# Rotary step of a decoder-trunk kernel: the partner rows added by accumulating transfers of the Pool queue

## Chip, cores and metric

The kernel runs on one core of a Trainium2 chip. The metric is the device time of one execution in microseconds (us). Each time below is that of the whole program: one layer of gated linear attention, one layer of dilated attention, two feed-forward blocks, for 1024 prompt tokens and 32 sample tokens.

## What is computed

The part that matters is the rotary step of keys and queries. Each head is a vector of 128 numbers per token. After its RMS norm, the first 32 of the 128 are rotated in pairs (number a with number a + 16) by an angle that depends on the token's position; the other 96 stay as they are.

```python
def rope_partial(x, pos):
    half = ROPE_DIM // 2                      # 16
    ...
    x1 = xf[..., :half]
    x2 = xf[..., half:ROPE_DIM]
    out = jnp.concatenate([x1 * cos - x2 * sin, x2 * cos + x1 * sin, xf[..., ROPE_DIM:]], axis=-1)

def dilated_mixer(h, w_q, q_norm, w_o, pos, attend):
    q = (h @ w_q).reshape(B, L, N_GROUPS, N_KV, Q_PER_KV, HEAD_DIM)
    q = rope_partial(rms_norm(q, q_norm), pos)
    for g, (win, dil) in enumerate(DIL_GROUPS):
        o, l = attend(q[:, :, g], win, dil)
```

Four key heads and 24 query heads (3 groups g of 8) are rotated this way, 28 heads in all. The rest of the trunk (projections, softmax, feed-forward) is not touched.

## The kernel before

Activations stand transposed: a tile has 128 partitions (features) and T = 1056 columns (1024 prompt tokens, 32 sample tokens), all float32. A projection of one head is 24 matmuls for each third of the columns (CW = 352): eight weight blocks, each as high and low part in three products (`proj`, L929 and L271).

`qk_head` (L793) finishes a head. For each third it scales the product (L829), squares it (L831), splits the square (L135), sums it over the partitions by two matmuls with ones (L800, L801), takes the reciprocal root by Ln and Exp on ScalarE (L802, L803), and writes the normed head on VectorE (L805). Heads of the groups g > 0 are written by L809 in class order: token 4u + r goes to column 256r + u, since the dilated attention works on the four classes r of the tokens; L813 writes the 32 sample columns. Then `rotate` (L815) turns the first 32 partitions, in four VectorE operations on 32 x 1056 elements: a shuffle that fetches the partner rows (L817), the product of the partner with the sine table (L818), the product of the head with the cosine table (L819), and the sum (L820). The tables are loaded by `rope_table` (L837): one in token order for keys and group 0, one in class order for groups 1 and 2, made on the host.

The steps of `qk_head` are put into a list `late` and run one third later, so a head's rotation is written while the next head is projected.

`mixer` (L1142 and on) runs eight slots s. In a slot, `attend(s)` (L957) takes the three queries q[0], q[1], q[2] of the slot:

- eight near-by scores of q[0] (L973) with their masked softmax parts on VectorE (L966) and exponentials on ScalarE,
- eight dilated scores (L984), each from q[1] and q[2], with the same softmax part (L966),
- weights that go through DRAM and back (L1005, L1007), transposes and products with the values (L1018 to L1056).

Score tiles come from a pool of two PSUM buffers (`sc`, L893): a score's matmul waits until the softmax part two scores before it has read its buffer. The queries of slot s + 1 are projected in between. After every second slot `sample` (L1069 and on) does the sample tokens' attention, from `Qs`, into which GpSimd copies the sample columns of each head (`sample_part`, L943).

Each engine does its instructions in a fixed order that a list scheduler of the framework sets when the program is built, from its own estimate of each operation's duration. A change of one operation thus also changes the place of others.

Names in the rows: `hs` is the temporary of `rotate`, `q` and `kh` are the heads, `tab` the tables, `p_s` the score tiles, `pA` and `pB` the near-by and dilated softmax tiles, `p_n` the sum of squares, `mm` a projection, `htl` and `hth` the low and high part of the square.

Of the kernel before, what the change touches and what calls it, by code (L numbers as in the profile page):

```python
# [8 lines left out]
F32 = mybir.dt.float32  # L9
# [4 lines left out]
ALU = mybir.AluOpType  # L14
# [4 lines left out]
NP, NS = 1024, 32  # L19
T = NP + NS  # L20
# [15 lines left out]
def yoco_step_kernel(  # L36
# [6 lines left out]
    nc = tc.nc  # L43
# [8 lines left out]
    class Turns:  # L52


        def __init__(self, *pools):
            self.pools, self.n = list(pools), 0
# [45 lines left out]
    def gcol(i):  # L102
        return gt[:, i:i + 1]

    G_A, G_F, G_E, G_KV, G_B, G_ON, G_K, G_Q, G_GK = 0, (8, 16), (24, 32), 40, 48, 56, 58, 59, 60

    XH, XL = [], []
# [24 lines left out]
    def split(hi, lo, x, g=None):  # L132
        if g is None:
            nc.scalar.copy(hi, x)  # L134
            nc.vector.tensor_tensor(lo, x, hi.bitcast(F32), op=ALU.subtract)  # L135
        else:
            nc.scalar.activation(hi, x, AF.Copy, scale=g)
            nc.vector.scalar_tensor_tensor(lo, x, g, hi.bitcast(F32), op0=ALU.mult, op1=ALU.subtract)  # L138
# [116 lines left out]
    def wtile(src, kt=8):  # L255
        raw = raws.tile([128, 1024], F32, tag="raw", name="raw")
        hi = wp.tile([128, 8, 128], F32R, tag="whi", name="whi")
        lo = wp.tile([128, 8, 128], F32R, tag="wlo", name="wlo")
        n = kt * 128
        nc.sync.dma_start(raw[:, :n], src)  # L260
        split(*(t[:].rearrange("p k m -> p (k m)")[:, :n] for t in (hi, lo)), raw[:, :n])
        return hi, lo
# [526 lines left out]
    def ln_exp_set():  # L789
        return tc.keep_in_program_order(nc.scalar.preload_act_table_set("natural_log_exp_and_others"))  # L790


    def qk_head(chunks, g, tab, tp, dst, pre, late, classes=False, early=False):  # L793
        def flush():
            while late:
                late.pop(0)()

        def finish(s, q, t, th, tl):
            p = sm.pools[0].tile([128, CW], F32, tag="sm", name="p_n")
            nc.tensor.matmul(p, ones_r, th, start=True, stop=False)  # L800
            nc.tensor.matmul(p, ones_r, tl, start=False, stop=True)  # L801
            nc.scalar.activation(t, p, AF.Ln, scale=1.0 / 128, bias=epsb)  # L802
            nc.scalar.activation(t, t, AF.Exp, scale=-0.5)  # L803
            if not classes:
                nc.vector.scalar_tensor_tensor(dst[:, s], q, g, t, op0=ALU.mult, op1=ALU.mult)  # L805
                return
            e = min(s.stop, NP) - s.start
            u = slice(s.start // 4, (s.start + e) // 4)
            nc.vector.scalar_tensor_tensor(  # L809
                dst[:, :NP].rearrange("p (r u) -> p u r", r=4)[:, u], q[:, :e].rearrange("p (u r) -> p u r", r=4), g,  # L810
                t[:, :e].rearrange("p (u r) -> p u r", r=4), op0=ALU.mult, op1=ALU.mult)
            if e < CW:
                nc.vector.scalar_tensor_tensor(dst[:, NP:], q[:, e:], g, t[:, e:], op0=ALU.mult, op1=ALU.mult)  # L813

        def rotate():  # L815
            t = tp.tile([64, T], F32, tag="hs", name="hs")
            nc.vector.stream_shuffle(t[32:64], dst[:32], [(a + 16) % 32 for a in range(32)])  # L817
            nc.vector.tensor_tensor(t[:32], t[32:64], tab[32:64], op=ALU.mult)  # L818
            nc.vector.tensor_tensor(dst[:32], dst[:32], tab[:32], op=ALU.mult)  # L819
            nc.vector.tensor_tensor(dst[:32], dst[:32], t[:32], op=ALU.add)  # L820

        for c, ps in chunks:
            flush()
            s = slice(c * CW, (c + 1) * CW)
            q, t, th, tl = (tp.tile([128, CW], F32R if n in ("hth", "htl") else F32, tag=n, name=n, bufs=3 if n == "hq" else 2)
                            for n in ("hq", "ht", "hth", "htl"))
            if early:
                nc.scalar.copy(q, ps)
            nc.vector.tensor_tensor(q, q if early else ps, rstd[:, s], op=ALU.mult)  # L829
            with tc.issue_after(pre.ins):  # L830
                nc.scalar.activation(t, q, AF.Square)  # L831
            split(th, tl, t)
            late.append(lambda a=(s, q, t, th, tl): finish(*a))
        late.append(rotate)
        return flush

    def rope_table(pool, i=0):  # L837
        tab = pool.tile([64, T], F32, name=f"tab{i}")
        nc.sync.dma_start(tab, c_rope[i])
        return tab  # L840


    def shared_kv(X, ssq, tp):
# [35 lines left out]
        return mq  # L879

    def to_class(ap):
        return ap.rearrange("p (u r) -> p r u", r=4)

    class Mixer:
        def __init__(self, st, mq):
            def pool(name, bufs, **k):
                return st.enter_context(tc.tile_pool(name=name, bufs=bufs, **k))

            self.mq = mq
            self.po = sm.pools[1]
            self.sc = pool("sc", 2, space=PSUM, side="right")  # L893
            self.tr = pool("tr", 1, space=PSUM, side="right")
            p = self.pool = pool("mx", 1)
            self.mask_a = p.tile([128, 256], F32, name="mask_a")
            self.mask_b = p.tile([128, 768], F32, name="mask_b")
            self.mask_s = p.tile([128, 656], F32, name="mask_s")
            self.Qs = [p.tile([128, 8, 32], F32, name=f"Qs{h}") for h in range(4)]
            self.kn = p.tile([128, 4, 32], F32, name="kn")  # L900
            self.os = p.tile([128, 8, 8, 4], F32, name="os")
            self.tab = [rope_table(p, i) for i in range(2)]
            self.head(0)
            self.pre = ln_exp_set()
            for h in range(4):
                nc.gpsimd.memset(self.Qs[h], 0.0)
# [33 lines left out]
        def queries(self, s):  # L940
            out, late = [], []

            def sample_part(g, q):  # L943
                nc.gpsimd.tensor_copy(
                    self.Qs[s // 2][:, :, g * 8 + s % 2 * 4:g * 8 + s % 2 * 4 + 4],
                    q[:, NP:].rearrange("p (b t) -> p b t", t=4))

            for g in range(3):
                q = self.pool.tile([128, T], F32, tag="q", name="q", bufs=QB)
                flush = qk_head(self.proj(wtile(w_q[3 * s + g]), XH, XL), gcol(G_Q), self.tab[g > 0], self.pool, q,  # L950
                                self.pre, late, classes=g > 0)
                late.append(lambda g=g, q=q: sample_part(g, q))
                out.append(q)
            flush()
            return out
# [234 lines left out]
    X, ssq, tp = block(0, xp, X, H_, L_, Od[7], w_oa, pick0)  # L1190
# [4 lines left out]
    xp, op, X = mixer(mq)  # L1195
# [141 lines left out]
```

## Time and profile before

| | us |
|---|---|
| median of 3 runs | 2961.36 (2958.55 to 2965.35) |
| profiled execution, device time | 2967.59 |
| its span, first to last instruction | 2965.8 |
| TensorE (PE) busy | 2909.5 |
| VectorE (DVE) busy | 1845.1 |
| ScalarE (ACT) busy | 1085.1 |
| GpSimd (POOL) busy | 19.9 |

The span is the time between the first and the last instruction; 1.8 us of the device time lie around it. Engines work side by side, so busy times do not add up to the span. The row of an engine tells how long it had something in work; a wait row tells how long it had nothing, and which other engine's result or which transfer ended that. PEld is TensorE's loading of weights, which runs beside the matmuls. A "wait of PE" is time without a running matmul, a "wait of PEld" time without a running weight load, during which an earlier matmul may still run.

### The profile page before, as it was taken

Reading aid. Unit: us, or ns where it says so; the run is one execution under the profiler, and the core shown is the slowest. Engines: PE = TensorE matmul, PEld = TensorE weight load, DVE = VectorE, ACT = ScalarE, POOL = GpSimd, SP = SyncE. Lnnn points to the kernel's source line nnn. Section 1 sums busy time; section 2 is a strip of 40 time slices with the busy share of each in tenths; the row PEclk is TensorE's granted clock in tenths of the full one; section 3 lists DMA queues with packets and bytes.
Section 4 is the critical chain, followed back from the end, with each engine's and each line's share of the span. In section 5 each row is a group of like instructions: output and inputs, shape, how many; then the busy total and the mean of one; then the engine's idle time right before and its main releaser. Section 6 shows DMA issues by size and latency. Waiting matters only on the chain.

```text
span 2965.8 us, 47230 instructions
## 1 busy us (share of the span) xinstructions
PE 2909.5 (98%) x19920; PEld 2762.0 (93%) x19920; DVE 1845.1 (62%) x2769; ACT 1085.1 (37%) x1761; POOL 19.9 (1%) x44
## 2 busy tenths in 40 slices
PE   8999999999999999999999999999999999999999
PEld 7889898899999999999988879788899999999999
DVE  6345455776766544467687778784676666654364
ACT  5233333522222221235455555552532222231141
POOL 0000000000000000000000000000000000000000
PEclk9999999999999999999999999999999999999999
DMA  3121234322222442132433141334422222262123
GB/s 129 59 74 51 74 140 142 119 80 80 81 72 87 171 129 74 41 127 102 132 91 107 59 122 44 115 107 134 167 79 73 87 72 80 76 237 75 50 77 110
DMA packets 133987, 291.06 MB, mean 98 GB/s; under 512 B 34160, under 2 KB 58736, under 8 KB 132752
## 3 DMA queue, kind: packets, MB, share of 16 engines
q1 hardware_dynamic: 133040, 287.72, 29.4%
q8 instruction: 157, 2.57, 0.4%
q14 instruction: 54, 0.44, 0.1%
q10 hardware_dynamic: 736, 0.33, 0.0%
HBM read 216.14 MB, written 71.86 MB: 97 GB/s over the span
## 4 chain that ended last, share of the span: by engine, by line
PE 88%; DVE 6%; DMA 3%; ACT 2%; issue 1%; SPq 0%; DVEq 0%; ACTq 0%
PE mm L271 38%; PE be L207 13%; PE ga L207 9%; PE al L207 8%; PE mm L937 6%; PE mm L671 2%; PE p_s L984 1%; PE p_o L1052 1%; PE mm L289 1%; DMA vv<-in_cv_dram 1%; DMA kk<-in_ck_dram 1%; DVE hs L817 1%; DVE q L809 1%; PE p_s L973 1%; DVE q L819 1%
## 5 line engine op out<-in xcount | busy, mean ns | idle before, releaser
L134 ACT CAST whi<-raw 128x1024 fp32r<-128x1024 f32 (+2 forms) x244 | 197.6, 810 | 789.3 <-PE mm L271 578.5
L135 DVE TENSOR_TENSOR wlo<-raw,whi 128x1024 fp32r<-128x1024 f32 (+2 forms) x244 | 224.6, 921 | 80.0 <-ACT whi L134 79.9
L764 DVE TENSOR_TENSOR X<-mm,X 128x1056 f32<-128x1056 f32 (+1 forms) x100 | 121.1, 1213 | 235.7 <-PE mm L271 235.5
L271 PE MATMUL mm<-XH,wlo 128*128 128x352 f32 x1104 | 245.3, 328 | 4.7 <-DVE wlo L135 4.7
L271 PE MATMUL mm<-XH,whi 128*128 128x352 f32 x1104 | 249.3, 331 | 0.2 <-ACT q_in L295 0.2
L271 PE MATMUL mm<-XL,whi 128*128 128x352 f32 x1104 | 247.3, 328 | 0.2 <-DVE XL L138 0.2
L134 ACT CAST hw<-S 128x512 fp32r<-128x512 f32 x176 | 108.8, 621 | 314.7 <-PE ga L207 181.8
L271 PE MATMUL mm<-GH,wlo 128*128 128x352 f32 x1038 | 223.6, 324 | 0.0
L271 PE MATMUL mm<-GL,whi 128*128 128x352 f32 x1038 | 223.6, 323 | 0.0
L271 PE MATMUL mm<-GH,whi 128*128 128x352 f32 x1038 | 223.3, 323 | 0.0
L207 PE MATMUL be<-Bh,hw 128*128 128x264 f32 x1056 | 216.6, 286 | 5.2 <-ACT hw L134 5.2
L207 PE MATMUL be<-Bl,hw 128*128 128x264 f32 x1056 | 215.8, 286 | 0.0
L207 PE MATMUL be<-Bh,lw 128*128 128x264 f32 x1056 | 214.9, 285 | 0.0
L271 PEld LDWEIGHTS mm<-XH,wlo 128*128 128x128 f32 x1104 | 189.0, 190 | 8.0 <-DVE wlo L135 5.3
L271 PEld LDWEIGHTS mm<-XH,whi 128*128 128x128 f32 x1104 | 188.6, 189 | 8.2 <-issue 3.1
L271 PEld LDWEIGHTS mm<-XL,whi 128*128 128x128 f32 x1104 | 190.2, 189 | 4.1 <-issue 1.3
L937 PE MATMUL mm<-XL,whi 128*128 128x352 f32 x576 | 193.7, 336 | 0.0
L937 PE MATMUL mm<-XH,whi 128*128 128x352 f32 x576 | 193.7, 336 | 0.0
L937 PE MATMUL mm<-XH,wlo 128*128 128x352 f32 x576 | 189.3, 329 | 0.0
L271 PEld LDWEIGHTS mm<-GL,whi 128*128 128x128 f32 x1038 | 177.0, 188 | 0.3 <-DVE GL L135 0.2
L271 PEld LDWEIGHTS mm<-GH,whi 128*128 128x128 f32 x1038 | 176.6, 188 | 0.0
L271 PEld LDWEIGHTS mm<-GH,wlo 128*128 128x128 f32 x1038 | 176.5, 189 | 0.0
(342 smaller groups left out, 6292.9 us busy)
## 6 DMA issues: line engine op xcount, KB each, us to landing
raw<-in_w_fi_dram SPq DMA_DIRECT2D x88, 512.0 KB, 3.5
Gd<-g SPq DMA_DIRECT2D x44, 528.0 KB, 2.7
gr<-Gd SPq DMA_DIRECT2D x44, 528.0 KB, 4.9
raw<-in_w_fo_dram SPq DMA_DIRECT2D x64, 256.0 KB, 2.7
raw<-in_w_a_dram SPq DMA_DIRECT2D x24, 512.0 KB, 3.5
raw<-in_w_q_dram SPq DMA_DIRECT2D x24, 512.0 KB, 3.7
kk<-in_ck_dram SPq DMA_DIRECT2D x40, 256.0 KB, 3.5
vv<-in_cv_dram SPq DMA_DIRECT2D x40, 256.0 KB, 2.9
```

Of the source, the lines that this page charges most:

```text
L134: nc.scalar.copy(hi, x)
L135: nc.vector.tensor_tensor(lo, x, hi.bitcast(F32), op=ALU.subtract)
L207: nc.tensor.matmul(ps[:, c, :HC], a[:, k, :], b[:, c * HC:(c + 1) * HC], start=(first and k == 0 and i == 0), stop=(k == len(xs) - 1 and i ...
L271: nc.tensor.matmul(ps[:, c, :CW], a[:, k, :], b[k][:, c * CW:(c + 1) * CW], start=(k == 0 and i == 0), stop=(k == n - 1 and i == 2),)
L289: nc.tensor.matmul(ps, a[:, k, :], b[k][:, s], start=(k == 0 and i == 0), stop=(k == n - 1 and i == 2))
L671: nc.tensor.matmul(ps[:, c, :CW], raw[:, 128 * k:128 * k + 128], ps_[k][:, c * CW:(c + 1) * CW], start=(k == 0), stop=(k == 1))
L764: nc.vector.tensor_tensor(like(X[m], s, p), p, like(X[m], s, p), op=ALU.add)
L809: nc.vector.scalar_tensor_tensor(dst[:, :NP].rearrange("p (r u) -> p u r", r=4)[:, u], q[:, :e].rearrange("p (u r) -> p u r", r=4), g, t[: ...
L817: nc.vector.stream_shuffle(t[32:64], dst[:32], [(a + 16) % 32 for a in range(32)])
L819: nc.vector.tensor_tensor(dst[:32], dst[:32], tab[:32], op=ALU.mult)
L937: nc.tensor.matmul(ps, a[:, k, :], b[k][:, s], start=(k == 0 and i == 0), stop=(k == n - 1 and i == 2))
L973: nc.tensor.matmul(ps[:, :n], q[0][:, j * 128:(j + 1) * 128], self.KA[:, k0:k0 + n], start=True, stop=True)
```

## The change

`rotate` keeps two VectorE products: partner table times head into `t`, and cosine table times head in place. The sum over the partner rows is made by two transfers of the Pool queue: rows 16 to 31 of `t` are added to rows 0 to 15 of the head, and rows 0 to 15 of `t` to rows 16 to 31. For that the sine table is loaded with its two halves swapped. The shuffle and the VectorE sum go. There is one table, in token order; heads in class order read it with a step of four columns, in one product of 1024 columns, and the 32 sample columns get a product of their own.

```diff
         def rotate():
-            t = tp.tile([64, T], F32, tag="hs", name="hs")
-            nc.vector.stream_shuffle(t[32:64], dst[:32], [(a + 16) % 32 for a in range(32)])
-            nc.vector.tensor_tensor(t[:32], t[32:64], tab[32:64], op=ALU.mult)
-            nc.vector.tensor_tensor(dst[:32], dst[:32], tab[:32], op=ALU.mult)
-            nc.vector.tensor_tensor(dst[:32], dst[:32], t[:32], op=ALU.add)
+            t = tp.tile([32, T], F32, tag="hs", name="hs")
+            for d, tb, own in ((t, tab[:, 1], False), (dst, tab[:, 0], True)):
+                if classes:
+                    nc.vector.tensor_tensor(*(x[:32, :NP].rearrange("p (r u) -> p r u", r=4) for x in (d, dst)),
+                                            to_class(tb[:, :NP]), op=ALU.mult)
+                    nc.vector.tensor_tensor(d[:32, NP:], dst[:32, NP:], tb[:, NP:], op=ALU.mult)
+                else:
+                    nc.vector.tensor_tensor(d[:32], dst[:32], tb, op=ALU.mult)
+            for i in range(2):
+                nc.gpsimd.dma_start(dst[16 * i:16 * i + 16], t[16 - 16 * i:32 - 16 * i], accum_op=ALU.add)
...
-    def rope_table(pool, i=0):
-        tab = pool.tile([64, T], F32, name=f"tab{i}")
-        nc.sync.dma_start(tab, c_rope[i])
+    def rope_table(pool):
+        tab = pool.tile([32, 2, T], F32, name="tab")
+        nc.sync.dma_start(tab[:, 0], c_rope[0, :32])
+        for i in range(2):
+            nc.sync.dma_start(tab[16 * i:16 * i + 16, 1], c_rope[0, 48 - 16 * i:64 - 16 * i])
         return tab
+
+    def to_class(ap):
+        return ap.rearrange("p (u r) -> p r u", r=4)
...
-            self.tab = [rope_table(p, i) for i in range(2)]
+            self.tab = rope_table(p)
...
-                flush = qk_head(self.proj(wtile(w_q[3 * s + g]), XH, XL), gcol(G_Q), self.tab[g > 0], self.pool, q,
+                flush = qk_head(self.proj(wtile(w_q[3 * s + g]), XH, XL), gcol(G_Q), self.tab, self.pool, q,
```

In the changed file the lines after `rotate` have other numbers: L966 becomes L975, L973 L982, L984 L993, L937 L946; the products are L820 (class order), L822 (sample columns) and L824, the transfers L826.

The scheduler also places other instructions differently. VectorE's order in slot s = 1, about the rotation of its last head q[2], before (`q_14134` is q[2]; the rows L966 with `pA` are the last near-by softmax parts):

```order
L966 ISA pA_14304,stA_14278<-p_s_14302,mask_a_13243 128x256
L966 ISA stA_14278 128x1
L809 SCALAR_TENSOR_TENSOR q_14134<-hq_14218,gt_72,ht_14219 128x88x4
L966 ISA pA_14309,stA_14278<-p_s_14307,mask_a_13243 128x256
L966 ISA stA_14278 128x1
L966 ISA pA_14314,stA_14278<-p_s_14312,mask_a_13243 128x256
L966 ISA stA_14278 128x1
L966 ISA pA_14319,stA_14278<-p_s_14317,mask_a_13243 128x256
L966 ISA stA_14278 128x1
L809 SCALAR_TENSOR_TENSOR q_14134<-hq_14257,gt_72,ht_14258 128x80x4
L813 SCALAR_TENSOR_TENSOR q_14134<-hq_14257,gt_72,ht_14258 128x32
L817 STREAM_SHUFFLE hs_14272<-q_14134 32x1056
```

The same place now (`q_14140` is q[2]):

```order
L975 ISA pA_14319,stA_14288<-p_s_14317,mask_a_13245 128x256
L975 ISA stA_14288 128x1
L809 SCALAR_TENSOR_TENSOR q_14140<-hq_14265,gt_72,ht_14266 128x80x4
L813 SCALAR_TENSOR_TENSOR q_14140<-hq_14265,gt_72,ht_14266 128x32
L820 TENSOR_TENSOR hs_14280<-q_14140,tab_13254 32x1024
L822 TENSOR_TENSOR hs_14280<-q_14140,tab_13254 32x32
L975 ISA pA_14324,stA_14288<-p_s_14322,mask_a_13245 128x256
L975 ISA stA_14288 128x1
L820 TENSOR_TENSOR q_14140<-q_14140,tab_13254 32x1024
L822 TENSOR_TENSOR q_14140<-q_14140,tab_13254 32x32
L975 ISA pA_14329,stA_14288<-p_s_14327,mask_a_13245 128x256
L975 ISA stA_14288 128x1
```

Before, all eight near-by softmax parts stood ahead of the rotation of q[2]. Now the last of the head's norm and the two products stand ahead of the seventh and the eighth part (`p_s_14322`, `p_s_14327`). Slots 0 to 6 have this order; slot 7, which has no next queries to project, has its own.

TensorE's order in the same slot, from the eighth near-by score (`p_s_14327`) to the first dilated score of q[1] (`p_s_14333`, `q_14010`), now:

```order
L982 MATMUL p_s_14327<-KA_13258,q_13892 128x256
L946 MATMUL mm_14724<-XH4_13203,whi_14719 128x352
L946 MATMUL mm_14724<-XL4_13211,whi_14719 128x352
L946 MATMUL mm_14724<-XH4_13203,wlo_14720 128x352
L946 MATMUL mm_14724<-XH5_13204,whi_14719 128x352
L946 MATMUL mm_14724<-XL5_13212,whi_14719 128x352
L946 MATMUL mm_14724<-XH5_13204,wlo_14720 128x352
L946 MATMUL mm_14724<-XH6_13205,whi_14719 128x352
L946 MATMUL mm_14724<-XL6_13213,whi_14719 128x352
L946 MATMUL mm_14724<-XH6_13205,wlo_14720 128x352
L946 MATMUL mm_14724<-XH7_13206,whi_14719 128x352
L946 MATMUL mm_14724<-XL7_13214,whi_14719 128x352
```

One more projection matmul follows, then `p_s_14333`; eight projection matmuls further stands the second dilated score of q[1] (`p_s_14340`), and after 26 more and two norm matmuls (L800, L801) the first score of q[2]. Before, the first score of q[1] followed the eighth near-by score at once, the second came three projection matmuls later, and the first of q[2] after 34 more and two norm matmuls.

The Pool queue, which held only copies in the mixer, now reads there (`x2` counts the two transfers of a head):

```order
L826 DMA q_13892<-hs_14048 16x1056 x2
L953 COPY Qs0_13248<-q_13892 128x8x4
L826 DMA q_14010<-hs_14179 16x1056 x2
```

Each copy of sample columns stands behind its head's two transfers and now waits for their landing.

## Rows read from the trace of the kernel before

**Rows 1.** The page's first part: busy us, share of the span, instructions.

```profile
PE 2909.5 (98%) x19920; PEld 2762.0 (93%) x19920; DVE 1845.1 (62%) x2769; ACT 1085.1 (37%) x1761; POOL 19.9 (1%) x44
```

**Rows 2.** Busy time by stretch: stretch, length, PE, PEld, DVE, ACT, POOL, clock, DMA, GB/s.

```profile
1330.00:1400.00 70.00, 70.00 (x426) 68.65 (x426) 51.17 (x55) 37.07 (x50) 0.00 (x0) 1.00 0.29 98
1473.00:2010.00 537.00, 511.08 (x3475) 453.02 (x3475) 417.22 (x1022) 290.76 (x701) 17.20 (x32) 0.99 0.32 94
```

**Rows 3.** Waits, 1473 to 2010 us: engine and line, what ended it, total, times, longest.

```profile
PEld p_s L973 <- DVE stA L966: 9.1, 22, 1.3
...
PEld p_n L801 <- DVE htl L135: 4.7, 12, 1.3
...
PE p_s L973 <- DVE stA L966: 3.1, 7, 0.9
PE mm L937 <- DVE OL L135: 3.0, 2, 2.6
...
PEld p_s L984 <- DVE q L820: 2.3, 6, 0.4
...
PE p_n L801 <- DVE htl L135: 1.2, 2, 1.0
```

**Rows 4.** DVE groups by shape: line, operation, shape, count; busy us, mean ns; idle before.

```profile
L818 DVE TENSOR_TENSOR hs<-hs,tab 32x1056 f32<-32x1056 f32 x28 | 34.9, 1247 | 0.9
L817 DVE STREAM_SHUFFLE hs<-q 32x1056 f32<-32x1056 f32 x24 | 32.2, 1343 | 0.6
...
L820 DVE TENSOR_TENSOR q<-q,hs 32x1056 f32<-32x1056 f32 x24 | 29.8, 1242 | 0.1
...
L809 DVE SCALAR_TENSOR_TENSOR q<-hq,gt,ht 128x352 f32<-128x352 f32 x32 | 27.4, 856 | 6.3 <-ACT ht L803 6.3
...
L966 DVE CUSTOM_DVE_ANT_0 pA<-p_s,mask_a 128x256 f32<-128x256 f32 x56 | 22.3, 419 | 6.7 <-PE p_s L973 6.7
...
L805 DVE SCALAR_TENSOR_TENSOR q<-hq,gt,ht 128x352 f32<-128x352 f32 x24 | 13.7, 576 | 2.0 <-ACT ht L803 2.0
...
L809 DVE SCALAR_TENSOR_TENSOR q<-hq,gt,ht 128x320 f32<-128x320 f32 x16 | 12.7, 795 | 8.5 <-ACT ht L803 8.5
...
L813 DVE SCALAR_TENSOR_TENSOR q<-hq,gt,ht 128x32 f32<-128x32 f32 x16 | 3.7, 229 | 0.0
```

**Rows 5.** Lines L427 and L428, copies in steps of 64 and 4 columns: ns min/median/max.

```profile
L427 DVE COPY dec<-cum x4: 171/176/178, 52.6 to 328.5; 128x16 f32<-128x16 f32 x4
...
L428 DVE COPY dec<-cum x4: 164/164/166, 52.6 to 328.6; 128x8 f32<-128x8 f32 x4
```

**Rows 6.** ACT groups, 1380 to 2075 us: a write in steps of four columns, a plain one.

```profile
L1030 ACT COPY o<-p_o 128x512 f32<-128x512 f32 x16 | 17.4, 1087 | 1.6 <-PE p_o L1028 1.1
...
L1043 ACT COPY pta<-p_t 128x512 f32<-128x512 f32 x24 | 14.3, 594 | 16.4 <-PE p_t L1041 16.3
```

**Rows 7.** The chain that ended last, 1555 to 1566 us: start, us, what.

```profile
1556.90 3.87 PE mm L937 x24
```

**Rows 8.** Timeline of slot 1: PE at its last near-by scores, DVE at q[2]'s sum.

```profile
1579.98 0.70 PE L973 MATMUL p_s<-KA,q 128*128 128x256 f32 x2
1580.51 0.38 PE L984 MATMUL p_s<-KB,q 128*128 128x128 f32 x2
...
1586.78 1.24 DVE L820 TENSOR_TENSOR q<-q,hs 32x1056 f32<-32x1056 f32 x1
```

**Rows 9.** DMA issues: transfer, issuing queue, count, KB each, median us to landing.

```profile
x<-in_x_t_dram SPq DMA_DIRECT2D x8, 528.0 KB, 9.0
...
raw<-in_w_ep_dram SPq DMA_DIRECT2D x16, 128.0 KB, 2.2
```

**Rows 10.** Busy time by stretch, as in rows 2: four us in slot 1.

```profile
1608.00:1612.00 4.00, 2.62 (x14) 1.79 (x13) 2.56 (x14) 0.76 (x2) 0.00 (x0) 0.68 0.12 42
```

**Rows 11.** Lines L989 (DVE) and L921 (the Pool copy `KB`): ns min/median/max.

```profile
L989 DVE TENSOR_TENSOR pB<-pB x64: 281/416/1675, 1530.8 to 2003.3; 128x128 f32<-128x128 f32 x32, 128x256 f32<-128x256 f32 x32
...
L921 POOL COPY KB<-KA x4: 2048/2052/2162, 1490.0 to 1865.7; 128x1024 f32<-128x1024 f32 x4
```

More of the change, by code (lines that the diff above doesn't have):

```diff
@@ L879, in shared_kv @@
         return mq
-    def to_class(ap):
-        return ap.rearrange("p (u r) -> p r u", r=4)
     class Mixer:
```

## The prediction

> **What bounds the kernel now.** I read the page's head first, then the busy time by stretch, then the waits of the stretch in which the rotations stand, and the timeline of one slot last.
>
> TensorE is busy for 98% of the span, 2909.5 us, VectorE for 62% [rows 1]. So time can only come from TensorE's waits. The keys are rotated in a stretch in which PE is busy for 70.00 of 70.00 us and DVE for 51.17 [rows 2]: there four rotations on DVE cost nothing now, and making them shorter gains nothing. All that the change can move lies between 1473 and 2010 us, where the 24 query heads are rotated: PE is busy for 511.08 of 537.00 us there, its weight loads for 453.02, and DVE for 417.22 [rows 2].
>
> The waits of that stretch that end with VectorE are short and many. Scores wait for the softmax part that frees their PSUM buffer (L966): 3.1 us of PE in 7 waits, and 9.1 us of PEld in 22. The first dilated score waits for the rotation's sum (L820): 2.3 us in 6. The norm matmul waits for the square's low part: 1.2 us of PE, 4.7 us of PEld. The output projection waits for its split: 3.0 us in 2 [rows 3]. A PEld wait can lie under a matmul that still runs, so it bounds a loss and does not show one. The rotation is thus mostly hidden already: in slot 1 q[2]'s sum runs from 1586.78 us on for 1.24 us, some six us after the first dilated score of q[1] at 1580.51 [rows 8], and PE has projected meanwhile.
>
> **The change, part by part.** *What VectorE is spared.* A rotation now is a shuffle of 1.343 us, two products of 1.247 and a sum of 1.242 [rows 4], 5.08 us; I take both products at L818's time. In token order two products remain: 2.49 us, 2.59 less. That holds for the 4 key heads and the 8 heads of group 0.
>
> The 16 heads in class order read the table in steps of four columns. The trace has no VectorE product with such a read. The lower bound is no penalty: 1.247 x 1024 / 1056 = 1.21 us. Near rows: L809, which writes a head in steps of 256 columns, takes 856 ns where L805 writes it plainly in 576 [rows 4], 1.49 times as long, which would be 1.80 us. L427 reads 16 columns in steps of 64 in 176 ns, L428 8 columns in 164 [rows 5]: 8 more columns cost 12 ns, 1.5 ns each, and 1024 of them, with the 0.16 us of the small copy for what is fixed, make 1.70. The upper bound is ScalarE's write in steps of four: 1087 ns against 594 [rows 6], 1.83 times, which gives 2.21. I take P = 1.70, since L427 is the same engine's read, and L809's factor lies beside it. [...]
>
> Each sample-column product is taken as L813's 0.23 us [rows 4]. A class-order rotation is then 2 x (1.70 + 0.23) = 3.86 us, 1.22 less than now. In the mixer DVE is spared 8 x 2.59 + 16 x 1.22 = 40 us of its 417, most of it where it waits anyway.
>
> *Waits that go.* The 2.3 us for L820 go, as that sum is no longer DVE's. Of the scores' 3.1 us and the norm's 1.2 us I take half, 1.5 and 0.6, as only some of them stand behind a rotation. The output split stands behind the last rotation now, and the order puts it ahead of it; of its 3.0 us I take 2.6, the time of shuffle and sum. Together **-7.0 us**. The least is the 2.3; the most, all rows 3, 23.4.
>
> *Waits that come from the new order.* In slots 0 to 6 the tail of q[2]'s norm and both products stand ahead of the seventh and eighth near-by softmax part. The first dilated score needs the seventh's PSUM buffer, the second the eighth's. Count from the end of the sixth part. DVE has L809's last third 0.80, L813 0.23, then P, 0.23, and the softmax part 0.42: 1.68 + P [rows 4]. PE has the eighth near-by score, 0.70, and 12 projection matmuls at 3.87 / 24 = 0.161 us [rows 7, 8], 1.93: together 2.63. The first wait is P - 0.95. From there DVE needs P + 0.23 + 0.42, PE 0.38 and 8 x 0.161 [rows 7, 8] = 1.67: the second is P - 1.02. A slot gets 2P - 1.97 us: 1.43 at P = 1.70, 0.45 at 1.21, 2.45 at 2.21. Seven slots: **+10.0 us**, between 3.2 and 17.2. Slot 7 is left at nothing: its order also has the split ahead.
>
> *The two transfers.* Queued behind them on Pool is only the head's copy of sample columns, and those are read after the score that waits for the same landing. q[0] and q[1] have a third of a head or more (24 matmuls, 3.87 us [rows 7], and the near-by scores) before they are read. q[2] is the tight one. From its last product, DVE does the eighth softmax part (0.42), PE the second dilated score (0.70) and 28 matmuls at 0.161, 4.51: a cover of 5.6 us. No transfer of the Pool queue, and no adding one, is in the trace. The nearest in size (128 KB against 66 KB) lands in 2.2 us, the slowest load in 9.0 [rows 9]. I take two in a row at 2 x 2.2 = 4.4 us, hidden: **0**. The upper end, 9.0, would cost 3.4 us in each slot. [...]
>
> *The rest.* The key heads' stores now wait for landings; the mixer reads keys only after four value projections, some 60 us later by the stretch in rows 2. The tables are three smaller loads instead of one, issued ahead of use. Both cost nothing; without that cover a landing would cost once.
>
> **The sum** is -7.0 + 10.0 + 0 = +3 us. Made against the profiled execution that is 2967.6 + 3 = 2970.6; that execution lies 6.2 us above the median of the three runs, 2961.4, so the median should come out at 2964.4. A measurement of this kernel can tell about 0.2% from no change, 5.9 us: I forecast no difference that can be told.
>
> **Rivals.** *Faster.* The table read costs nothing extra (P = 1.21) and half of the PEld waits of L973 and L801 were real: -7.0 - 6.9 + 3.2 = -10.7, 2951. For it: DVE is busy for 78% of the mixer [rows 2]. Against: PE is at 95% there. Chance 0.18.
>
> *Slower: the transfers land late.* One mechanism in one place, the first score of q[2]. It decides from 5.6 us for the pair; beyond that every us costs PE one in each of 7 slots, at 9.0 us 24 us more than the sum: 2988. For it: Pool's queue makes two transfers one after the other, and both want the same engines as the weight loads. Against: row 2.2 us. Chance 0.15.
>
> *Slower: the clock.* [...] Chance 0.12.
>
> *Slower: Pool and VectorE hold each other up.* A DVE sum of 281 ns took 1675 [rows 11] at most, 1.39 us more, and Pool's copy of 2.05 us is the only long thing that Pool does in the mixer. If the issue of each transfer did that, a slot would get up to 2.8 us more: 2984. [...] Chance 0.05.
>
> *The change does not spare what it says.* At P = 2.21 a class-order rotation is 4.88 us against 5.08, and the order costs 17.2: 2961.4 + 10.2 = 2972. Chance 0.08.
>
> **How the numbers follow.** No difference 0.42, at 2964.4; faster 0.18; slower 0.15 + 0.12 + 0.05 + 0.08 = 0.40. The range reaches down to 2950, past the faster case, and up to 2988, where the late transfers at their dearest lie; what is left out is the rest of both ends, some 0.2. The forecast's own range is 2957 to 2967.
>
> **What would show it.** Right: PE waits at the first two dilated scores of q[1] for the softmax part, about 0.7 us each; L820 at 1.7 us a product; no wait for a Pool transfer at the first score of q[2]; the split's wait gone. Wrong: a product near 1.2 us or above 2.2; a pair of transfers over 5.6 us; PE waits that end with a transfer into q; a clock below 0.97 in the slots.

## The result, and the profile after

The changed kernel takes 2980.75 us (median of 4 runs, 2978.56 to 2983.4); the kernel before, run beside it, 2962.22 us (4 runs, 2958.55 to 2965.35). The ratio is 1.0053, with a 95% interval of 1.0041 to 1.0066. The time lies in the range that was given, but the interval leaves out 1: the kernel is slower, by 18.5 us between the medians, where no difference was forecast.

The profiled execution took 2983.4 us, 15.8 more than that of before. The head of its page, which answers to [rows 1]:

```profile
span 2981.6 us, 47387 instructions
PE 2912.3 (98%) x19920; PEld 2763.4 (93%) x19920; DVE 1803.9 (61%) x2717; ACT 1086.9 (36%) x1761; POOL 63.6 (2%) x100
```

VectorE has 41 us less to do, ten of it for the four key heads (4 x 2.59); the mixer's share is some 31, where 40 was forecast. PE still has its 98%: the loss is in short waits once more. Busy time by stretch, as in [rows 2], of the kernel before:

```profile
1473.00:1950.00 477.00, 458.60 (x3137) 406.99 (x3136) 370.27 (x909) 261.80 (x632) 15.60 (x29) 1.00 0.30 87
1990.00:2000.00 10.00, 9.97 (x46) 8.90 (x44) 6.69 (x22) 5.13 (x14) 1.18 (x1) 0.74 0.83 303
```

and of the changed kernel:

```profile
1473.00:1950.00 477.00, 447.50 (x3068) 395.44 (x3067) 332.63 (x830) 252.42 (x605) 48.91 (x71) 1.00 0.35 92
2000.00:2020.00 20.00, 13.45 (x48) 11.52 (x49) 10.68 (x26) 8.14 (x19) 1.75 (x3) 0.66 0.78 214
```

Up to 1950 us, some six slots, PE works 11.1 us less in the same time. Worked out from the two traces, the first near-by score of slot 7 starts 16.1 us later than before (1992.7 against 1976.6) and the mixer's last product (`p_o`) 20.1 us later (2064.5 against 2044.4). Behind that, where the change does nothing, this profile took 4.3 us less (917.1 against 921.4); the profiles of all kernels here lie between 917.0 and 921.6 there, so this is scatter. Who waits now is in the waits of PE from 1473 to 2075 us (total, times, longest), which answer to [rows 3]. The lines are numbered anew: L966 is now L975, L973 is L982, L984 is L993, L937 is L946, and L826 issues the transfers.

```profile
PE p_s L993 <- DMA q<-hs: 11.4, 8, 4.0
PE p_s L993 <- DVE stA L975: 7.1, 11, 1.2
PE p_n L801 <- DVE htl L135: 4.2, 6, 0.8
...
PE p_s L993 <- issue: 2.7, 4, 0.7
PE p_s L982 <- DVE stA L975: 2.4, 2, 1.9
...
PE mm L946 <- DVE OL L135: 0.2, 1, 0.2
```

Three kinds are new. Dilated scores wait for landings of the transfers into `q`: 11.4 us in 8 waits, one in each slot. They wait for near-by softmax parts: 7.1 us in 11, and the 2.7 us in 4 are the same place in slots 0, 2, 4 and 6. The norm matmul waits for the low part: 4.2 us where it was 1.2. Gone are the wait for the rotation's sum (L820, a PEld row of [rows 3]) and that for the output's split, 3.0 us, of which 0.2 is left.

The products by form, from the VectorE groups that answer to [rows 4]:

```profile
L820 DVE TENSOR_TENSOR q<-q,tab 32x1024 f32<-32x1024 f32 x16 | 31.9, 1996 | 0.0
L820 DVE TENSOR_TENSOR hs<-q,tab 32x1024 f32<-32x1024 f32 x16 | 31.8, 1986 | 0.0
...
L824 DVE TENSOR_TENSOR q<-q,tab 32x1056 f32<-32x1056 f32 x8 | 10.0, 1246 | 0.2
...
L822 DVE TENSOR_TENSOR q<-q,tab 32x32 f32<-32x32 f32 x16 | 2.8, 172 | 0.0
```

Slot 1 in order of time, around q[2]'s rotation; PE rows of the projection are left out:

```profile
1586.55 1.99 DVE L820 TENSOR_TENSOR hs<-q,tab 32x1024 f32<-32x1024 f32 x1
...
1588.57 0.40 DVE L975 CUSTOM_DVE_ANT_0 pA<-p_s,mask_a 128x256 f32<-128x256 f32 x1
...
1588.91 2.00 DVE L820 TENSOR_TENSOR q<-q,tab 32x1024 f32<-32x1024 f32 x1
1589.04 0.49 PE L993 MATMUL p_s<-KB,q 128*128 128x128 f32 x2 [0.61 <-DVE stA L975]
1590.85 0.17 DVE L822 TENSOR_TENSOR q<-q,tab 32x32 f32<-32x32 f32 x1
1590.95 0.41 DVE L975 CUSTOM_DVE_ANT_0 pA<-p_s,mask_a 128x256 f32<-128x256 f32 x1
...
1591.42 0.70 PE L993 MATMUL p_s<-KB,q 128*128 128x256 f32 x2 [0.60 <-DVE stA L975]
1591.59 1.54 POOL L826 DMA_DIRECT2D q<-hs  x2 [9.24 <-DVE stA L975]
1592.03 0.38 SPq L986 DMA_DIRECT2D scr<-stA  x1
...
1597.72 0.21 POOL L953 COPY Qs<-q 128x32 f32<-128x32 f32 x1 [4.59 <-DMA q<-hs]
```

This is the order the prediction worked with: product, seventh softmax part, product, eighth part, and each of the first two dilated scores (1589.04 and 1591.42) waits 0.6 us for one of those parts. The pair of transfers is issued in 1.54 us, up to 1593.13; the copy of sample columns, which waits for the same landing, starts 4.59 us after that. During the two issues SP's queue sends the row maxima and row sums of the near-by scores to DRAM (`scr<-stA`, below called the store of row maxima).

### The profile page after: what moved, and what is told of

Read it like the earlier page. It is cut to its first block, busy times and chain, and to the rows that moved or that the text cites. A ratio compares the mean times of both kernels' runs of the same rounds, so it can differ in the third digit from the quotient of the medians.

```text
span 2981.6 us, 47387 instructions
## 1 busy us (share of the span) xinstructions
PE 2912.3 (98%) x19920; PEld 2763.4 (93%) x19920; DVE 1803.9 (61%) x2717; ACT 1086.9 (36%) x1761; POOL 63.6 (2%) x100
## 4 chain that ended last, share of the span: by engine, by line
PE 70%; DVE 4%; DMA 3%; ACT 1%; issue 1%; POOL 0%; SPq 0%; DVEq 0%
PE mm L271 26%; PE be L207 12%; PE ga L207 8%; PE al L207 8%; PE mm L946 7%; DMA q<-hs 2%; PE p_s L993 1%; PE p_o L1061 1%; PE mm L671 1%; DVE hs L820 1%; PE mm L289 1%; DMA vv<-in_cv_dram 1%; PE p_n L801 1%; PE p_s L982 1%; DVE q L820 0%
## 5 line engine op out<-in xcount | busy, mean ns | idle before, releaser
L134 ACT CAST whi<-raw 128x1024 fp32r<-128x1024 f32 (+2 forms) x244 | 198.2, 812 | 810.3 <-PE mm L271 584.5
L134 ACT CAST hw<-S 128x512 fp32r<-128x512 f32 x176 | 109.2, 623 | 311.8 <-PE ga L207 178.6
L946 PE MATMUL mm<-XL,whi 128*128 128x352 f32 x576 | 192.9, 335 | 0.0
L946 PE MATMUL mm<-XH,whi 128*128 128x352 f32 x576 | 192.6, 334 | 0.0
L946 PE MATMUL mm<-XH,wlo 128*128 128x352 f32 x576 | 192.3, 334 | 0.0
```

The lines of the kernel that those rows point to most:

```text
L946: nc.tensor.matmul(ps, a[:, k, :], b[k][:, s], start=(k == 0 and i == 0), stop=(k == n - 1 and i == 2))
```

## What the experiments tell apart

My theory ahead of the runs (A) was the list of waits above: product length, lateness of the transfers and new order each had a part in the loss. The rivals put all of it on the transfers (B) or all on the read in steps (C).

**The table read straight.** The heads in class order read the one table as it stands in memory, so they are rotated by the numbers of other columns and the kernel tells the time alone.

```diff
-                if classes:
-                    nc.vector.tensor_tensor(*(x[:32, :NP].rearrange("p (r u) -> p r u", r=4) for x in (d, dst)),
-                                            to_class(tb[:, :NP]), op=ALU.mult)
-                    nc.vector.tensor_tensor(d[:32, NP:], dst[:32, NP:], tb[:, NP:], op=ALU.mult)
-                else:
-                    nc.vector.tensor_tensor(d[:32], dst[:32], tb, op=ALU.mult)
+                nc.vector.tensor_tensor(d[:32], dst[:32], tb, op=ALU.mult)
```

> The heads in class order read the table in place order, without steps; which part is changed: their rotation uses the numbers of other columns. The transfers stay. Theory A (the loss of 18.5 us is three kinds of wait: some 1.5 us per slot at the first two dilated scores of q[1] because products of 2.0 us stand ahead of softmax parts, some 0.95 us per slot of the norm matmul for the low part, 1.2 us per slot and 4.2 us in slot 7 for the landing of q[2]'s transfers): products fall to 1.24 us, the two waits of q[1] to under 0.3 us each, the low part's to under 0.4 us, and the wait for the landing stays at 1.0 to 1.5 us; 2966 to 2970 us. Rival B (the transfers alone make the loss): 2976 us or more. Rival C (the read in steps alone makes it): 2963 us or less.

2952.16 us; ratio to before 0.9962 (0.9951 to 0.9974). It is 28.6 us faster than the changed kernel and, with its transfers, 10.8 us faster than the kernel before. Its waits of PE, 1473 to 2075 us (line numbers shift with each edit: the dilated score is L988 here, the softmax part L970):

```profile
PE p_s L988 <- DMA q<-hs: 3.1, 1, 3.1
PE p_s L988 <- DVE stA L970: 1.8, 2, 1.0
...
PE p_n L801 <- DVE htl L135: 0.2, 1, 0.2
```

The wait for the landing is left in slot 7 alone; in the other seven it went too, which theory A had not expected, and the time is 14 us below A's range. C's number came out, B is done with.

**The read in steps in the kernel before.** One table, products in steps of four; shuffle and sum stay on VectorE, no transfers.

```diff
-            nc.vector.tensor_tensor(t[:32], t[32:64], tab[32:64], op=ALU.mult)
-            nc.vector.tensor_tensor(dst[:32], dst[:32], tab[:32], op=ALU.mult)
+            for d, x, tb in ((t[:32], t[32:64], tab[32:64]), (dst[:32], dst[:32], tab[:32])):
+                if classes:
+                    nc.vector.tensor_tensor(*(a[:, :NP].rearrange("p (r u) -> p r u", r=4) for a in (d, x)),
+                                            tb[:, :NP].rearrange("p (u r) -> p r u", r=4), op=ALU.mult)
+                    nc.vector.tensor_tensor(d[:, NP:], x[:, NP:], tb[:, NP:], op=ALU.mult)
+                else:
+                    nc.vector.tensor_tensor(d, x, tb, op=ALU.mult)
```

> The kernel before with only the table changed: heads in class order read the one table in steps of four, shuffle and sum stay on VectorE, no transfers. Theory A: products of 2.0 us, a rotation of about 7.0 us against 5.1, VectorE 27 us busier, and the first score of q[2] waits for the rotation's sum 1.5 to 1.8 us in each slot where it waited 0.25: 2970 to 2976 us. Rival B (the read in steps costs nothing on the path): 2961 to 2965 us.

2986.55 us; ratio 1.0075 (1.0058 to 1.0092), 23.6 us more than before and 10 above the top of what was expected. The place was wrong: the first score of q[2] does not wait for the sum. The waits of PE in the same stretch:

```profile
PE p_n L801 <- DVE htl L135: 12.0, 7, 1.9
PE p_s L978 <- DVE stA L971: 11.6, 8, 2.6
...
PE mm L942 <- DVE OL L135: 4.4, 2, 4.2
```

Against 1.2, 3.1 and 3.0 us in [rows 3] that is 20.7 us more, all from work that stands behind a long product on VectorE: the low part of the norm's square, a near-by softmax part, the output's split. A product has several followers, and the prediction counted one kind of them. The order of instructions moved in this kernel too, so these rows do not tell length and order apart.

**No transfers of the query heads** (`for i in range(2)` around the issue becomes `range(2 if tp.name == 'kvp' else 0)`); their partner rows are not added.

> The changed kernel without the transfers of the query heads: their partner rows are not added; those of the keys are. Theory A: the waits for landings (1.2 us in seven slots, 4.2 in the last) go, some of it to waits for the products themselves, and the waits of q[1]'s scores stay: 2968 to 2973 us. Rival C (the read in steps alone makes the loss, so the waits only change their name): 2978 us or more. Rival B (the transfers alone): 2963 us or less.

2968.37 us; ratio 1.0019 (1.001 to 1.0029), in A's range: 12.4 us less than the changed kernel. Without a landing to wait for, the order puts the first scores of q[2] right behind the products, and some waits change their name (`PE p_s L993 <- DVE q L820` totals 4.2 us in 7). So this tells what the transfers cost with the best order without them, beside long products.

**The table in class order.** The same single table, loaded from the class-order half of the constant, so that q[0] now reads in steps, of 256 columns, and 16 heads read straight. Nothing is left out.

```diff
-            self.tab = rope_table(p)
+            self.tab = rope_table(p, 1)
...
-                if classes:
-                    nc.vector.tensor_tensor(*(x[:32, :NP].rearrange("p (r u) -> p r u", r=4) for x in (d, dst)),
-                                            to_class(tb[:, :NP]), op=ALU.mult)
+                if tabc and not classes:
+                    nc.vector.tensor_tensor(*(x[:32, :NP].rearrange("p (u r) -> p u r", r=4) for x in (d, dst)),
+                                            tb[:, :NP].rearrange("p (r u) -> p u r", r=4), op=ALU.mult)
```

> The changed kernel with the mixer's one table held in class order, so that only q[0] reads it in steps (of 256 columns) and q[1] and q[2] read it straight; nothing left out. Theory A: as with the plain read but for q[0], whose products, of 1.8 to 2.0 us, have a third of a head of cover: 2966 to 2971 us. Rival C: half of the heads that read in steps, half of the loss, about 2971 us. Rival B: 2976 us or more.

2954.29 us; ratio 0.9966 (0.9955 to 0.9977). **This is faster than both kernels**: 8.7 us under the one before, 26.5 under the changed one, and 11.7 under the lowest time that was expected. Its products:

```profile
L824 DVE TENSOR_TENSOR q<-q,tab 32x1056 f32<-32x1056 f32 x16 | 19.9, 1244 | 0.3
...
L820 DVE TENSOR_TENSOR q<-q,tab 32x1024 f32<-32x1024 f32 x8 | 15.8, 1978 | 0.0
```

A step of 256 columns costs what a step of four does, 1978 against 1996 ns, but only q[0] pays it. Half of the loss was not left, as C had it, but 2 us of 28.6, within the scatter of the runs: eight long products of q[0] have their cover.

**Length or order?** The straight read had moved softmax parts ahead of the products (its order differs in a few places), so length and order had changed together. Here the straight read keeps the two pieces of the changed kernel's product, and with them its order of instructions on PE and VectorE, row for row.

```diff
-                    nc.vector.tensor_tensor(*(x[:32, :NP].rearrange("p (r u) -> p r u", r=4) for x in (d, dst)),
-                                            to_class(tb[:, :NP]), op=ALU.mult)
+                    nc.vector.tensor_tensor(d[:32, :NP], dst[:32, :NP], tb[:, :NP], op=ALU.mult)
```

> The changed kernel with its two pieces per product, and so with the same order of instructions on TensorE and VectorE throughout, but the table read straight; which part is changed: heads in class order are rotated by the numbers of other columns. Theory D (the length of the product makes the whole loss, the order nothing): as the plain read, 2950 to 2955 us, no wait over 0.3 us at the first scores of q[1] and q[2] in slots 0 to 6. Theory E (the order has a share: both products ahead of the last two softmax parts, and the row maxima's store, 1024 packets of 8 bytes, issued beside q[2]'s transfers): the waits at q[1] 0.2 to 0.3 us each, the wait for q[2]'s landing still 0.6 to 1.2 us, 2957 to 2964 us.

2960.2 us; ratio 0.9989 (0.998 to 0.9999). Theory E, as its numbers had it but for the waits at q[1], which went wholly in slots 0 to 6. Of the 28.6 us, 20.6 are the length of the product in an unchanged order; 8.0 are the order, together with the small products of the sample columns, which the straight read does not have. Product and remaining waits:

```profile
L820 DVE TENSOR_TENSOR q<-q,tab 32x1024 f32<-32x1024 f32 x16 | 19.3, 1207 | 0.0
```

```profile
PE p_s L992 <- DMA q<-hs: 8.1, 8, 1.8
...
PE p_s L992 <- DVE stA L974: 0.9, 1, 0.9
```

The landing is waited for in all eight slots although the products are short. In its slot 1 the pair and the store lie beside each other as in the changed kernel:

```profile
1582.88 1.54 POOL L825 DMA_DIRECT2D q<-hs  x2 [7.66 <-DVE stA L974]
1589.05 0.21 POOL L952 COPY Qs<-q 128x32 f32<-128x32 f32 x1 [4.62 <-DMA q<-hs]
```

```profile
1583.32 0.38 SPq L985 DMA_DIRECT2D scr<-stA  x1
```

With the table in class order the store goes out 1.1 us ahead of the pair, and the pair lands in half the time:

```profile
1582.52 1.54 POOL L826 DMA_DIRECT2D q<-hs  x2 [7.81 <-DVE hq L835]
1586.49 0.21 POOL L953 COPY Qs<-q 128x32 f32<-128x32 f32 x1 [2.42 <-DMA q<-hs]
```

```profile
1581.45 0.38 SPq L986 DMA_DIRECT2D scr<-stA  x1
```

**The store taken apart.** The changed kernel, with the row maxima of the first six softmax parts sent as soon as they are there.

```diff
-            nc.sync.dma_start(scr[:].rearrange("(j p) c -> p j c", p=128), stA)
+                if j in (5, 7):
+                    a = 0 if j == 5 else 6
+                    nc.sync.dma_start(scr[:].rearrange("(j p) c -> p j c", p=128)[:, a:j + 1], stA[:, a:j + 1])
```

> The changed kernel with the row maxima's store in two pieces, the first after the sixth softmax part, so that 256 and not 1024 small packets go out beside q[2]'s transfers; nothing left out. Theory E (the store delays the landing): from issue to landing 4.6 us fall to 3.5 or less, the wait for it from 1.2 us to under 0.5 in slots 0 to 6, 2972 to 2977 us. Theory D (the landing is late because the products are): 2979 to 2982 us.

2972.84 us; ratio 1.0033 (1.0022 to 1.0044): 7.9 us less than the changed kernel, with no instruction of VectorE moved and 6 of TensorE's 19920. The wait for the landing:

```profile
PE p_s L995 <- DVE stA L975: 7.6, 11, 1.6
...
PE p_s L995 <- DMA q<-hs: 2.5, 3, 1.4
```

11.4 us in 8 waits became 2.5 in 3; in slot 1 the copy follows the issue by 2.99 us instead of 4.59, though from issue to landing the median of its two transfers fell only from 4.6 to 3.9 us. In slots 0 to 6 it is 2.5 to 4.2 us instead of 4.4 to 4.8, and one wait, 0.64 us in slot 4, is over the 0.5 that was expected at most. The waits for softmax parts stay. Theory E is shown for slots 0 to 6 of this kernel: the store beside the pair made the landing late. What its packets are stands in the DMA view of the changed kernel, 1593 to 1594.5 us:

```profile
DMA packets 1026, 0.11 MB, mean 70 GB/s; under 512 B 1003, under 2 KB 1003, under 8 KB 1026
...
q0 software_dynamic: 42, 0.10, 59.9%
q1 hardware_dynamic: 984, 0.01, 37.7%
```

984 packets of SP's queue carry 0.01 MB and take 37.7% of the 16 engines while the transfers (q0) run. But that share is not what makes the landing late. Worked out from the trace, the pair's last packet ends at 1595.09 us, 1.96 us after the end of its issue; for q[1]'s pair in the same slot, with no store beside it, that is 1.77. The pair of q[1] has landed 0.34 us after its last packet, that of q[2] only 2.51 us after. For most of that time nothing moves (DMA view, 1596 to 1597.5 us), and SP's queue, which reads the store back (`stX<-scr`) when that has landed, does so just ahead of the copy of 1597.72:

```profile
DMA packets 0, 0.00 MB, mean 0 GB/s; under 512 B 0, under 2 KB 0, under 8 KB 0
```

```profile
1597.44 0.37 SPq L1002 DMA_DIRECT2D stX<-scr  x1
```

In slots 0 to 6 the pair's second landing follows the store's by 0.17 to 0.20 us, here and in the straight read with the same order. With the store in two pieces it follows the small one by 0.16 to 0.28, also in slots 3 and 4, where the small store itself lands late and the copy comes 3.9 and 4.2 us after the issue. So PE waits for the store's landing; why the pair's landing is noted only behind it, no run shows.

**Keys alone.** The kernel before, its four key heads rotated by transfers and nothing else.

> The kernel before with only the four key heads rotated by transfers. As predicted (TensorE is full there, nobody is waiting for the stores): 2960 to 2965 us. Rival, VectorE's spared 10 us count: 2957 us or less. Rival, the key heads' stores come late and the mixer's first head waits for its keys: 2966 us or more.

2963.24 us; ratio 1.0 (0.9991 to 1.0009), as predicted: neither the spared VectorE time nor the later stores count there.

**q[2] in two halves.** On the class-order table, q[2]'s products and transfers by halves of the columns, the half that is read first ahead.

```diff
+            if not far:
+                for s in (slice(0, 512), slice(512, T)):
+                    for d, a in ((t, 1), (dst, 0)):
+                        nc.vector.tensor_tensor(d[:32, s], dst[:32, s], tab[:, a, s], op=ALU.mult)
+                    for i in range(2):
+                        nc.gpsimd.dma_start(dst[16 * i:16 * i + 16, s], t[16 - 16 * i:32 - 16 * i, s], accum_op=ALU.add)
+                return
```

> The kernel with the table in class order, and q[2] rotated in two halves by columns, each with its own pair of transfers, so that the half that is read first lands first; nothing left out. If the landing in slot 7 (3.4 us of wait there) is what is left of the transfers' cost: that wait falls to 2 us or less, 2950 to 2954 us. Rival (four issues of 0.8 us in Pool's queue land the second half later than its first score): 2956 us or more.

2958.59 us; ratio 0.9983 (0.9974 to 0.9993): 4.3 us worse than the class table alone, and in the rival's range. The wait for the landing fell as hoped, but the order has all four half products ahead of the seventh softmax part, and in slot 7 PE waits at a near-by score (L989 here) instead; the second halves land late:

```profile
PE p_s L989 <- DVE stA L982: 2.9, 2, 2.4
...
PE p_s L1000 <- DMA q<-hs: 1.7, 2, 1.5
```

```profile
q<-hs POOLq DMA_DIRECT2D x16, 34.0 KB, 5.0
q<-hs POOLq DMA_DIRECT2D x16, 32.0 KB, 2.6
```

**Class table and store in pieces together.**

> Table in class order and the row maxima's store in two pieces, nothing left out: the two repairs together. If the store still stands beside q[2]'s transfers in slot 7, where 3.4 us are waited for the landing: that wait falls to 2 us or less and the time to 2949 to 2953 us. Rival (with short products the store has gone out already): 2953 to 2956 us, as with the class table alone.

2955.66 us; ratio 0.9974 (0.9965 to 0.9983), no better than the table alone, as the rival had it. Slot 7's wait for the landing is gone, and in its place PE waits 3.6 us for the output's split on ScalarE (`PE mm L946 <- ACT OH L134: 3.6, 1, 3.6`). The landing itself is still late there: the copy comes 6.15 us after the issue, 6.98 with the table alone. So in slot 7 the store is not all that makes it late; there the pair's own packets end late too, 5.1 us after its issue has ended (worked out from the trace), while two loads of 528 KB on SP's queue are under way. In slot 7 there is no next head to project, so whatever is late next shows.

**Straight read and no transfers.**

> Table read straight (class-order heads rotated by numbers of other columns) and no transfers of the query heads (their partner rows are not added). It tells what the transfers cost beside short products. Theory E: only slot 7's wait for the landing, 3.3 us, goes: 2947 to 2951 us. Rival (hidden landings cost nothing and earlier scores wait for the products): 2952 us or more.

2947.59 us; ratio 0.9948 (0.9933 to 0.9963): 4.6 us under the straight read with transfers. So beside short products the transfers cost some 5 us, beside long ones 12.4.

**Steps of two.** The changed kernel's order, `r=2` in place of `r=4` in both views of the product.

> The changed kernel with its order, the table read in steps of two columns; which part is changed: heads in class order are rotated by the numbers of other columns. [...] Rival (any step costs the same): 1.99 us, 2979 to 2983 us. Rival (a step of two costs nothing): 1.21 us, about 2960 us.

2959.11 us; ratio 0.9986 (0.9977 to 0.9995). The last rival came out, a step of two that costs nothing, to the nanosecond of the straight read:

```profile
L820 DVE TENSOR_TENSOR q<-q,tab 32x1024 f32<-32x1024 f32 x16 | 19.3, 1207 | 0.0
```

## Why the prediction was too low, point by point

**The waits from the new order: place right, size right by luck.** Forecast were about 0.7 us at each of the first two dilated scores; the rows of slot 1 have 0.61 and 0.60. In all, the 2.7 us and 7.1 us less slot 7's longest make 8.6 us in seven slots, where 10.0 stood. But the forecast took 1.70 us for a product: at the measured 1.99 its formula gives 1.04 and 0.97, 14 us in seven slots. It added whole durations, and the rows show the next VectorE instruction starting before the one ahead has ended (1588.91 against 1588.97), and 0.17 us, not 0.23, for a product of the sample columns.

**"I take P = 1.70": the step that failed most.** A product takes 1.99 us, 1.64 times the 1.21 of the same product read straight, which was the lower bound and is exact (1207 ns). With it VectorE was spared 31 us in the mixer and not 40. L809's factor of 1.49 and the copies L427 and L428 were both too kind; the factor 1.83 of ScalarE's write, taken as an upper end, was too harsh. By the prediction's own formula 0.29 us more is 4 us in seven slots; by the pair of kernels with one order 0.78 us of product is 20.6 us. So the price of a long product was mis-sized more than its length: the formula, 2P in each slot, counts the two scores of q[1] only, and their rows differ by 8.9 us between these two kernels. Followers that it left out: the norm's low part, 4.2 us of PE where a gain of 0.6 was taken, 0.2 with the short product; slot 7; and the landing, though by little (7.4 us of wait in slots 0 to 6, and 6.2 with the short product).

**"Hidden: 0" for the transfers: the second step that failed.** Its two halves came out one by one, the first by luck. The pair was taken as 4.4 us, two landings of 2.2 in turn; in the kernel with the straight read it is 0.56 us to the issue, 1.54 of issue and 2.28 to the copy, worked out from its slot 1, 4.4 us, but one transfer takes 3.2 (the median of 48) and the two overlap. The cover was taken as 5.6 us; in slot 1 from the last product's end (1591.02) to where PE stood ready (1597.73 less its wait of 1.11) it is 5.6. What was missing is the store of row maxima, which follows the eighth softmax part and so goes out within half a us of the pair, and behind whose landing the pair's is noted: 6.7 us from product to copy, and 1.1 us of wait. Rows of single transfers, such as [rows 9], could not show it; the order of SP's queue beside Pool's could have shown the store. That rival, late transfers at the first score of q[2], was named, with its threshold of 5.6 us, at a chance of 0.15; it is what happened, at 7.4 us in slots 0 to 6 of the 24 of its dearest price, and its reason, engines shared with the weight loads, was not the one there. Worked out from the trace of the changed kernel, the packets of the pair in slot 1 run one transfer after the other, but for 0.2 us: 1592.92 to 1594.28 and 1594.07 to 1595.09. Two other pairs, at 1629.54 and 1904.63, which have 1.09 and 1.23 MB of SP's queue beside them, move for 4.64 and 4.47 us, one with 0.47 MB for 1.99, and the pairs with no such load beside them for 1.8 to 2.2; those of q[2] in slots 0 to 6 are among these, with the store's small packets alone beside them.

**"Slot 7 is left at nothing": wrong, by some 4 us.** With no head to project, PE waits 1.9 us at a near-by score, 1.2 at the first of q[1] and 4.0 for the landing there. But in the kernel before it waited in that slot too, 5.5 us for softmax parts and the split. Worked out from the traces, the stretch from the slot's first score to the mixer's last product grew from 67.8 to 71.8 us, and PE's waits in it from 8.1 to 9.2. The granted clock goes with the rest: 0.66 for 20 us from 2000 on, 0.74 for 10 us from 1990 on before, part of each at 0.50 (2002 to 2007 us now, 1990 to 1995 before) and behind such waits (PE busy for 0.00 us from 2000 to 2001 and from 1988 to 1989); over the stretch, what the clock lacks to 1 makes 6.8 us, 3.4 before. In the keys-alone kernel, whose query heads are those of before, it makes 5.1, so a part of this is scatter. Of a slower clock, the rival at 0.12, slots 0 to 6 show nothing: it is 1.00 from 1473 to 1990 us.

**The waits that go: half of -7.0.** The 2.3 us for L820, counted whole, stand in a PEld row of [rows 3]; PE has no row of a wait for L820 before, so none of its time went with them. The split's 3.0 us fell to 0.2 and the 3.1 us of the near-by scores to 2.4, all of it in slot 7: 3.5 us in place of 4.1. The norm's 1.2 us grew to 4.2.

**What was right.** The keys at nothing. No Pool hold-up: L809's 352-column form takes 857 ns in the 9 times that it overlaps an issue of a transfer, 855 in the other 23, worked out from the trace.

**What the sum says at the right P.** At 1.21 us the prediction's terms make -7.0 + 3.2 = -3.8 us, and the kernel with the changed order and a product of 1.21 us came out 2.9 us under before. That agrees in part by two misses that cancel: 8.1 us of landings were taken at nothing, and the waits at q[1], 3.2 us by the formula, were none in slots 0 to 6. The faster rival, 2951 us at P = 1.21, is where the straight read came out (2952.16), but by another road: the rival counted on PEld waits in the changed order, and the straight read has another order.

**How the loss adds up.** New waits in the rows of PE, 1473 to 2075 us: 11.4 for landings, 9.3 more for softmax parts at dilated scores, 3.0 more for the low part: 24 us. Of the shorter ones the split and the near-by scores make 3.5; the others are waits for caches and for probabilities in the sample parts, which shift with every version. All rows together come to 25.4 us before and 39.4 now, 14.0 of the 15.8 us between the two profiled executions. The clock is no part of the loss: its mean over the runs is 0.9948 now and 0.995 in the runs of before. For the straight read and the class table it is 0.9961, so by estimate some 3 us of their gains are clock; why it rose was not taken apart.

What stays open: why the halves of q[2] cost 4.3 us. PE's rows in the mixer come to 16.1 us with them and 17.6 with the class table alone, so waits do not explain it. The mean clock is 0.9952 over ten runs against 0.9961 over seven, by estimate 2.7 us; the rest is not explained.

## What to carry to other kernels

A table that two orders share should lie in the order of the most and the latest readers; here turning the same table round made 8.7 us of gain out of 18.5 of loss. Cost a longer instruction by everything that stands behind it on its engine in each slot, not by the one follower that you found, and look at the last slot by itself, where nothing fills the waits. Before a transfer is called hidden, look which other queue issues a slow store in the same microsecond, and where that lands: here 8 KB landed 5.2 to 5.6 us after the start of their issue, in slots 0 to 6 of the changed kernel.

## What the hardware showed that I had not expected

A VectorE product of 32 x 1024 float32 whose table is read in steps of two columns takes 1207 ns, as when read straight; in steps of four 1996, in steps of 256 1978. Nothing is paid at a step of 8 bytes, and at 16 as much as at 1024. Why the price begins between the two, no run shows. A table that both orders read in steps of no more than two columns would by these times be free of it; none was tried.

The copy that waits for q[2]'s pair of accumulating transfers of 66 KB started 2.2 to 2.9 us after their issue ended in slots 0 to 6 with the straight read, where the store went out ahead of them, and 4.4 to 4.8 in those of the changed kernel, where the store of 8 KB in 8-byte packets was issued 0.4 to 0.7 us after the first transfer. There the pair's own packets had ended 2.4 to 2.8 us before its landing was noted, 0.17 to 0.20 us after the store's.
